# A feed-forward projection in Strassen block products: seven half-width products for eight in 28 of 32 feature tiles

## The chip, the cores and the metric

The kernel runs on one core of one Trainium2 chip. The metric is the device time of one execution in microseconds (us): 1504.65 us before, the median of three runs (1503.68 to 1504.9). Engines are called PE (TensorE matmul), PEld (its weight load), DVE (VectorE), ACT (ScalarE), POOL (GpSimd) and SP (SyncE, which issues the DMAs).

## The reference, cut to what matters

Two layers. Each has adaLN-modulated norms, an input projection, four token mixers and an output projection, and then an MLP with a gated residual. In layer 0 the MLP runs over 512 latent and 256 context tokens, in layer 1 over the 512 latent tokens alone.

```
def channel_mixer(h, w1, w2):          # w1: 1024 x 4096, w2: 4096 x 1024
    return jnp.square(jax.nn.relu(h @ w1)) @ w2

x = x + mod_x[5] * channel_mixer(modulate(rms_norm(x, norm2_g[l]), mod_x[3], mod_x[4]), mlp_w1[l], mlp_w2[l])
if l < DEPTH - 1:
    h_ctx = h_ctx + mod_c[5] * channel_mixer(..., mlp_w1[l], mlp_w2[l])
```

## The kernel before

Activations lie transposed: 128 features on the partitions, the 768 tokens (512 latent, 256 context) as columns. Every product is in fp32 accuracy by three fp32r matmuls (`mm3`, L683): weight high x activation high, weight high x activation low, weight low x activation high. A weight chunk is a 128 x 1024 tile (eight blocks of 128 x 128), loaded as `raw`, cast by ACT to its high part `wh` (L340) and subtracted by DVE to its low part `wl` (L302) in `weight_split` (L656). Three `wh`/`wl` pairs form a ring: the split of a chunk waits until PE has finished with the chunk three before it. Three `raw` tiles exist, two of them for these weights and one for adaLN rows.

`mlp` (L1658) goes over four groups of eight feature tiles of w1. A feature tile is 8 blocks x (512 + 256 columns) x 3 = 48 matmuls into one of two PSUM tiles of the kind `s` (two banks each); in group 0 the first three tiles go third by third (256 tokens each) as the norm delivers them (`together`, L712, names `pair`). `ev_ff` (L1644) takes a tile from PSUM: ReLU and square on ACT (`rl`), the high part `ffh` by a DVE cast (L320) and the low part `ffl` by a DVE subtraction. Then eight output tiles of w2, each over the group's eight `ff` tiles, and `residual` adds each to the stream `x` on DVE, 512 and 256 wide (L307). The last two output tiles of the last group go third by third, so that layer 1's first norm (`norm_third`: `sq`, `st`, `rs`, `rr`, `rb`, then `nu` and `hl` on DVE, `hh` on ACT) starts on third 0 while PE does thirds 1 and 2.

The order of all engines is fixed at build time: `Plan` runs the program's coroutines in a modelled time, and where several want an engine, the lower number in the table `PRIO` goes first. Each engine then executes its list in order. Beside the MLP run the adaLN rows (`ada_row`, `row_work`): a 128 x 1024 row is loaded and reduced on DVE (L594, `dump`) once or twice; those of part 5 of layer 0 (the MLP's gate) wait for the MLP's start (`LATE5 = 1`), the others of layer 1 follow, `ADA_GAP` apart.

Of the kernel before, what the change touches and what calls it, by code (L numbers as in the profile page):

```python
# [238 lines left out]
def hybrid_dit_kernel(  # L239
# [402 lines left out]
    def weight_loader():  # L642
        for i in range(len(order)):
            yield r_raw.get()
            raw = ring.tile([128, D], F32, tag="raw", bufs=N_RAW + N_ARAW, name="raw")
            t = dma(raw, order[i])
            P.spawn(weight_split(i, raw, t))
            while i - state["split"] > 1:
                yield state["split_ev"]
            if i == 1:  # L650
                yield a0_done

# [3 lines left out]
    def weight_split(i, raw, t):  # L656
# [1311 lines left out]
```

## Time and profile before

| | |
|---|---|
| median of three runs | 1504.65 us |
| the profiled execution | 1505.86 us |
| its span, first to last instruction | 1503.5 us (2.4 us lie outside) |
| mean granted TensorE clock | 0.991 |
| PE busy / DVE busy / ACT busy | 1471.1 / 930.6 / 542.2 us |

Busy time is a mean over stages, so it is read by stage: up to 224 us the start and layer 0's projections, to 392 its attention, output projection and first three MLP tiles, to 892 the rest of its MLP, to 924 the turn to layer 1, then the same again. A PE record lasts longer than the distance to the next one, since matmuls overlap; what a matmul costs in a stream is read from starts, or from a long stretch divided by its count. In the same way a DVE record lasts longer than the distance to the next one.

### The profile page before, as it was taken

The page shows a single profiled execution, that of the slowest core. Times are in us where ns is not written, and L with a number is a line of the kernel's source. Part 1 is how long each engine was busy: PE and PEld are TensorE (multiplying, and loading weights), DVE is VectorE, ACT ScalarE, POOL GpSimd, SP SyncE. Part 2 cuts the span into 40 slices and gives each one's busy share as a digit, 9 for nine tenths or more (in the row PEclk, how much of TensorE's full clock was granted, in tenths as well). Part 3 has the DMA queues.
Part 4 walks back from the last instruction along what each step waited for, and adds up shares of the span by engine and source line. Part 5 has one row for each costly group of instructions (what it writes and reads, how often), then busy time and mean ns, then how long its engine had stood idle before and what let it go on. Part 6 is the DMA issues. An engine that isn't in the chain of part 4 may idle for free.

```text
span 1503.5 us, 21831 instructions
## 1 busy us (share of the span) xinstructions
PE 1471.1 (98%) x8692; PEld 1254.8 (83%) x8692; DVE 930.6 (62%) x1631; ACT 542.2 (36%) x941; POOL 78.0 (5%) x94
## 2 busy tenths in 40 slices
PE   8999999999999999999999999999998999999997
PEld 5788887779888888888888899887778888888886
DVE  4899679769755565445443359999767434343343
ACT  4422337655421231132113235327645323132342
POOL 0000002220000000000000000102210000000000
PEclk8999999999999999999999999999999999999999
DMA  9563357211343444444441214545312333333331
GB/s 338 204 236 110 115 173 228 82 30 44 109 130 124 128 125 142 142 152 140 155 140 57 70 43 137 173 144 162 117 57 71 99 98 99 97 92 95 95 98 57
DMA packets 66758, 184.48 MB, mean 123 GB/s; under 512 B 8545, under 2 KB 15457, under 8 KB 66657
## 3 DMA queue, kind: packets, MB, share of 16 engines
q1 hardware_dynamic: 66656, 183.10, 38.0%
q8 instruction: 68, 1.11, 0.3%
q14 instruction: 34, 0.27, 0.1%
HBM read 168.91 MB, written 14.16 MB: 122 GB/s over the span
## 4 chain that ended last, share of the span: by engine, by line
PE 87%; DVE 8%; DMA 2%; issue 1%; SPq 1%; ACT 1%; POOL 0%; DVEq 0%; POOLq 0%; ACTq 0%
PE w L362 65%; PE wo L362 6%; PE pair L362 4%; PE tm L362 3%; PE pv L362 2%; PE tp L1179 2%; DVE wl L302 1%; PE score L362 1%; DMA a<-adaB 1%; DVE ca L307 1%; PE am L437 1%; SPq L368 1%; DVE e L1137 1%; DVE zr L302 1%; DVE x L307 1%
## 5 line engine op out<-in xcount | busy, mean ns | idle before, releaser
L340 ACT CAST wh<-raw 128x1024 fp32r<-128x1024 f32 x184 | 193.2, 1050 | 647.7 <-PE w L362 600.4
L362 PE MATMUL w<-hl,wh 128*128 128x512 f32 (+1 forms) x1072 | 380.1, 355 | 0.5 <-DVE hl L307 0.5
L362 PE MATMUL w<-hh,wh 128*128 128x512 f32 (+1 forms) x1072 | 379.8, 354 | 0.4 <-ACT hh L335 0.4
L362 PE MATMUL w<-hh,wl 128*128 128x512 f32 (+1 forms) x1072 | 378.1, 353 | 0.0
L302 DVE TENSOR_TENSOR wl<-raw,wh 128x1024 fp32r<-128x1024 f32 x184 | 225.0, 1224 | 214.1 <-ACT wh L340 211.1
L362 PE MATMUL w<-ffl,wh 128*128 128x512 f32 (+1 forms) x800 | 277.8, 347 | 0.0
L362 PE MATMUL w<-ffh,wh 128*128 128x512 f32 (+1 forms) x800 | 277.7, 347 | 0.0
L362 PE MATMUL w<-ffh,wl 128*128 128x512 f32 (+1 forms) x800 | 277.6, 347 | 0.0
L362 PEld LDWEIGHTS w<-hh,wh 128*128 128x128 f32 x1072 | 202.8, 189 | 30.5 <-issue 2.1
L362 PEld LDWEIGHTS w<-hl,wh 128*128 128x128 f32 x1072 | 202.8, 189 | 30.0 <-issue 3.0
L362 PEld LDWEIGHTS w<-hh,wl 128*128 128x128 f32 x1072 | 202.6, 189 | 27.2 <-issue 0.2
L307 DVE SCALAR_TENSOR_TENSOR x<-w,md,x 128x512 f32<-128x512 f32 (+1 forms) x100 | 62.1, 642 | 215.6 <-PE w L362 215.5
L362 PEld LDWEIGHTS w<-ffh,wh 128*128 128x128 f32 x800 | 151.5, 189 | 19.1
L362 PEld LDWEIGHTS w<-ffl,wh 128*128 128x128 f32 x800 | 151.5, 189 | 18.9
L362 PEld LDWEIGHTS w<-ffh,wl 128*128 128x128 f32 x800 | 151.4, 189 | 19.0
L594 DVE CUSTOM_DVE_ANT_0 dump<-raw,cbt 128x1024 bf16<-128x1024 f32 x80 | 97.6, 1220 | 19.3 <-DMA raw<-adaT 18.6
L307 DVE SCALAR_TENSOR_TENSOR ca<-gpad,sm,ca 128x783 f32<-128x783 f32 (+1 forms) x120 | 106.8, 890 | 2.3
L345 POOL TENSOR_TENSOR rr<-rs,few 128x2 f32<-128x2 f32 (+1 forms) x30 | 27.3, 911 | 1165.0 <-DVE rs L315 1165.0
L1137 DVE TENSOR_SCALAR_CACHE_REDUCE e<-score 128x768 f32<-128x768 f32 (+1 forms) x80 | 66.1, 846 | 21.5 <-PE score L362 21.2
L335 ACT ACTIVATE e<-e,mx 128x768 f32<-128x768 f32 (+1 forms) x80 | 67.8, 848 | 28.5 <-DVE e L1137 27.4
L362 PE MATMUL wo<-yl,wh 128*128 128x512 f32 (+1 forms) x144 | 53.5, 371 | 2.0 <-DVE yl L302 2.0
L302 DVE TENSOR_TENSOR ffl<-rl,ffh 128x512 fp32r<-128x512 f32 (+2 forms) x73 | 53.7, 742 | 2.1
(165 smaller groups left out, 1892.2 us busy)
## 6 DMA issues: line engine op xcount, KB each, us to landing
raw<-w SPq DMA_DIRECT2D x128, 512.0 KB, 3.6
raw<-adaT SPq DMA_DIRECT2D x56, 512.0 KB, 3.3
raw<-w_in SPq DMA_DIRECT2D x40, 512.0 KB, 4.1
ab<-adaB SPq DMA_DIRECT2D x24, 384.0 KB, 6.4
raw<-wo SPq DMA_DIRECT2D x16, 512.0 KB, 4.0
a<-adaB SPq DMA_DIRECT2D x16, 384.0 KB, 7.2
ks<-qk SPq DMA_DIRECT2D x48, 96.0 KB, 2.2
x<-xT SPq DMA_DIRECT2D x16, 256.0 KB, 5.3
```

The lines of the kernel that those rows point to most:

```text
L302: nc.vector.tensor_tensor(out=out, in0=in0, in1=in1, op=op)
L307: nc.vector.scalar_tensor_tensor(out=out, in0=in0, scalar=s, in1=in1, op0=op0, op1=op1)
L335: nc.scalar.activation(out=out, in_=in_, func=func, scale=scale, **kw)
L340: nc.scalar.copy(out, in_)
L345: nc.gpsimd.tensor_tensor(out=out, in0=in0, in1=in1, op=op)
L362: nc.tensor.matmul(out, lhsT, rhs, start=start, stop=stop)
L368: (eng or nc.sync).dma_start(out=out, in_=in_)
L437: nc.tensor.matmul(pm[32 * j:32 * j + 32, 0:256], sc4[:, j + (0 if first else 4)], raw, start=first, stop=last)
L594: nc.vector.tensor_tensor_reduce(out=dump, in0=raw, in1=cbt[s], op0=ALU.mult, op1=ALU.add, scale=1.0, scalar=0.0, accum_out=md[l][:, s, r: ...
L1137: nc.vector.tensor_scalar(out=e[:, 0:kn], in0=s_[:, k0:k0 + kn], scalar1=-SQ_D, scalar2=None, op0=ALU.mult, op1=ALU.min, accum_out=mx)
L1179: nc.tensor.transpose(tp[:, j * 128:(j + 1) * 128], e[0][:, (k3 + j) * 128:(k3 + j + 1) * 128], id_sb)
```

## The change

In layer 0, 28 of the 32 w1 tiles are taken two at a time. Of a pair, the 8 x 2 weight blocks are cut into four quarters (a11, a12 of one tile, a21, a22 of the other, 4 blocks each), the eight activation tiles and 768 tokens into four quarters of 4 tiles x 384 tokens. Strassen's scheme (in Winograd's form) gives the two feature tiles from seven products of 4 blocks x 384 columns x 3 = 12 matmuls; eight would be needed without sums. In exchange:

- `pair_split`: each pair's weights are four DVE sums of 128 x 512 and seven splits of 128 x 512, made from two raw tiles held at once. Seven halves lie in three and a half ring chunks.
- `sums`: once, during group 0, the activations' four summed quarters per block (`t1`, `t2`, `t3`), with their high and low parts. `t1` replaces the right half of the first four activation tiles after the four plain tiles (`plain_ev`).
- `seven_products`: products 1, 6, 2, 7, 5, 4, 3, each into half a PSUM tile, combined by an ACT copy and seven DVE additions 384 wide (`sum_q` to `sum_c12`); then ReLU, square and the cast to `ffh` on ACT, `ffl` on DVE (`squared`).
- Groups of layer 0 are 4, 6, 6, 6, 6, 4 tiles (`GROUPS`), so its w2 output is added to `x` six times, not four; group 0 is plain. After a group of pairs, the first two output tiles take all but the last two `ff` tiles first.
- Around it: part 5's adaLN rows no longer wait for the MLP (`LATE5 = 0`), `ADA_GAP`, `SLACK`, `CTX_LAG`, `H_KEEP`, the chunk order of both input projections (`W_ORDER`, two rows of number pairs) and nearly all of `PRIO` are different, and a weight's low part is always made on DVE.

```diff
+ADA_GAP = (7000.0, 6000.0, 9000.0, 4500.0, 5500.0)
...
+LATE5 = 0
...
+GROUPS = ((4, 6, 6, 6, 6, 4), (8, 8, 8, 8))
+HALF = NT // 2
...
+    def pair_loader(i, pairs):
...
+            for ap in p:
+                yield r_raw.get()
+                raw = ring.tile([128, D], F32, tag="raw", bufs=N_RAW + N_ARAW, name="raw")
+                two.append((raw, dma(raw, ap)))
+            got.append(two)
...
+            while not got:
+                yield more[0]
+            (r1, t1), (r2, t2) = got.pop(0)
+            a11, a12, a21, a22 = r1[:, 0:512], r1[:, 512:1024], r2[:, 0:512], r2[:, 512:1024]
+            yield t1
+            e11 = yield from half(a11)
+            yield t2
+            yield r_buf.get()
+            s1 = buf([128, 512], name="s1")
+            t = yield from v_tt(s1, a21, a22, ALU.add)
+            yield e11
+            yield from v_tt(a21, a11, a21, ALU.subtract)
+            yield t
+            t = yield from v_tt(a11, s1, a11, ALU.subtract)
+            yield t
+            e6 = yield from half(a11)
+            e12 = yield from half(a12)
+            yield r_buf.get()
+            s4 = buf([128, 512], name="s4")
+            t = yield from v_tt(s4, a12, a11, ALU.subtract)
+            P.spawn(put_after(r_raw, e6, e12, t))
+            yield from half(a21)
+            ev = yield from half(s1)
+            P.spawn(put_after(r_buf, ev))
+            ev = yield from half(a22)
+            P.spawn(put_after(r_raw, ev))
+            yield t
+            ev = yield from half(s4)
+            P.spawn(put_after(r_buf, ev))
...
+    def half_rest(c, o, src, wh, wl, last, ev):
+        t = yield from v_tt(wl, src, bits(wh), ALU.subtract)
+        P.fire(hev[c, o], t)
+        P.fire(ev, t)
...
+    def sums(L):
...
+            yield r_buf.get(2, True)
+            L.t2[k] = [buf([128, NT], F32R, name=nm) for nm in ("t2h", "t2l")]
+            yield r_buf.get(2)
+            u, v = buf([128, NT], name="su"), buf([128, NT], name="sv")
+            t1 = t1s[k // 2][:, (k % 2) * HALF:(k % 2 + 1) * HALF]
+            a, b = L.h2[k], L.h2[k + 4]
+            t = yield from v_tt(u, bits(a.hi), bits(a.lo), ALU.add)
+            tv = yield from v_tt(v, bits(b.hi), bits(b.lo), ALU.add)
+            yield t
+            t = yield from v_tt(t1, u[:, HI], u[:, LO], ALU.subtract)
+            yield max(t, tv)
+            t3 = yield from v_tt(u[:, HI], v[:, HI], u[:, HI], ALU.subtract)
+            t = yield from v_tt(v[:, HI], v[:, HI], t1, ALU.subtract)
+            yield t
+            t = yield from v_tt(v[:, LO], v[:, LO], v[:, HI], ALU.subtract)
+            yield t
+            h, lo = L.t2[k]
+            t = yield from a_copy(h, v)
+            h3, l3 = (x[:, (k % 2) * HALF:(k % 2 + 1) * HALF] for x in L.t3[k // 2])
+            t3 = yield from a_copy(h3, u[:, HI])
+            yield t
+            t = yield from v_tt(lo, v, bits(h), ALU.subtract)
+            for n in (2, 4):
+                P.fire(L.t_ev[k, n], t)
+            yield t3
+            t = yield from v_tt(l3, u[:, HI], bits(h3), ALU.subtract)
+            P.fire(L.t_ev[k, 3], t)
+            r_buf.put(2, t)
+        yield L.plain_ev
+        for k in range(4):
+            t1 = t1s[k // 2][:, (k % 2) * HALF:(k % 2 + 1) * HALF]
+            t = yield from a_copy(L.h2[k].hi[:, HI], t1)
+            yield t
+            t = yield from v_tt(L.h2[k].lo[:, HI], t1, bits(L.h2[k].hi[:, HI]), ALU.subtract)
+            P.fire(L.t_ev[k, 1], t)
+        r_buf.put(2, t)
+
...
+        LO, HI = slice(0, HALF), slice(HALF, NT)
+        h2 = L.h2
+        yield L.sums_ev
+        third = lambda k: slice((k % 2) * HALF, (k % 2 + 1) * HALF)
...
+        def product(p, out):
+            if at["n"] % 2 == 0:
+                at["c"] = chunk()
...
+            yield hev[c, o]
+            wh, wl = wt_[c]
+            for k in range(4):
+                if p in waits:
+                    yield L.t_ev[k, waits[p]]
+                hi, lo = token[p](k)
+                t = yield from mm3(out, wh[:, 4 * o + k], wl[:, 4 * o + k], hi, lo, k == 0, k == 3)
+            if o or at["n"] == 7 * (len(ff) // 2):
+                free_ring(c)
...
+            S.left = {ff[i]: 2, ff[i + 1]: 2}
+            yield r_s.get()
+            p_ = acc_tile("s", "sa")
+            S.a, S.b = p_[:, 0:HALF], p_[:, 512:512 + HALF]
+            yield r_buf.get()
+            S.x = buf([128, NT], name="sx")
+            t = yield from product(1, S.a)
+            P.spawn(sum_p(S), t)
+            t = yield from product(6, S.b)
+            P.spawn(sum_q(S), t)
+            yield r_buf.get(3, True)
+            S.y = buf([128, NT], name="sy")
+            ff[i].make("ff")
+            yield r_acc.get()
+            S.g = acc_tile("acc", "sg")[:, 0:HALF]
+            t = yield from product(2, S.g)
+            P.spawn(sum_c11(S, ff[i]), t)
+            yield r_s.get()
+            p_ = acc_tile("s", "sb")
+            S.c, S.d = p_[:, 0:HALF], p_[:, 512:512 + HALF]
+            t = yield from product(7, S.c)
+            P.spawn(sum_r(S), t)
+            t = yield from product(5, S.d)
+            yield r_buf.get(3, True)
+            S.z = buf([128, NT], name="sz")
+            ff[i + 1].make("ff")
+            P.spawn(sum_c22(S, ff[i + 1]), t)
+            yield r_acc.get()
+            S.e = acc_tile("acc", "sc")[:, 0:HALF]
+            t = yield from product(4, S.e)
+            P.spawn(sum_c21(S, ff[i + 1]), t)
+            yield r_acc.get()
+            S.h = acc_tile("acc", "sh")[:, 0:HALF]
+            t = yield from product(3, S.h)
+            P.spawn(sum_c12(S, ff[i]), t)
+
...
+    def sum_q(S):
+        yield S.ev["p"]
+        t = yield from v_tt(S.x[:, HALF:NT], S.b, S.x[:, 0:HALF], ALU.add)
+        r_s.put(1, t)
...
+    def sum_r(S):
+        yield S.ev["q"]
+        yield S.ev["y"]
+        t = yield from v_tt(S.x[:, 0:HALF], S.c, S.x[:, HALF:NT], ALU.add)
...
+    def sum_c22(S, f):
+        yield S.ev["r"]
+        t = yield from v_tt(S.z[:, HALF:NT], S.d, S.x[:, 0:HALF], ALU.add)
+        P.spawn(rectified(S, S.z, HALF, f), t)
+        t = yield from v_tt(S.x[:, HALF:NT], S.d, S.x[:, HALF:NT], ALU.add)
+        r_s.put(1, t)
+        P.fire(S.ev["u"], t)
...
+    def squared(S, y, o, f):
+        y = y[:, o:o + HALF]
+        t = yield from act(y, y, AF.Square)
+        yield t
+        t = yield from a_copy(f.hi[:, o:o + HALF], y)
+        yield t
+        t = yield from v_tt(f.lo[:, o:o + HALF], y, bits(f.hi[:, o:o + HALF]), ALU.subtract)
+        S.left[f] -= 1
+        if not S.left[f]:
+            r_buf.put(1, t)
+        P.fire(f.ev[0 if o == 0 else 2], t)
+        if not S.left[f]:
+            P.fire(f.ev[1], t)
...
+                cs = [chunk()] if m or not (seven and g) else [chunk(), chunk()]
+                ps = {}
+                cuts = [0, nf] if len(cs) == 1 else [0, nf - 2, nf]
+                for k0, k1 in zip(cuts, cuts[1:]):
+                    for j, c in enumerate(cs):
+                        if c not in ps:
+                            yield wev[c]
```

How this moves instructions, at three places. On PE, at the end of layer 0's group 0, before: the last w1 tile (`w1_4718`) ends and the first w2 output tile begins; the w2 rows run over eight `ff` tiles, of which these are the first three.

```order
L362 MATMUL w1_4718<-hl_4124,wh_4585 128x256
L362 MATMUL w1_4718<-hh_4123,wl_4586 128x256
L362 MATMUL w2_4783<-ffh_4016,wh_4652 128x512
L362 MATMUL w2_4783<-ffl_4017,wh_4652 128x512
L362 MATMUL w2_4783<-ffh_4016,wl_4653 128x512
L362 MATMUL w2_4783<-ffh_4018,wh_4652 128x512
L362 MATMUL w2_4783<-ffl_4019,wh_4652 128x512
L362 MATMUL w2_4783<-ffh_4018,wl_4653 128x512
L362 MATMUL w2_4783<-ffh_4020,wh_4652 128x512
```

The same place on PE now; `w1_4492` is the tile that becomes `ffh_4490` and `ffl_4491`.

```order
L364 MATMUL w1_4492<-hl_4163,wh_4449 128x256
L364 MATMUL w1_4492<-hh_4162,wl_4450 128x256
L364 MATMUL w2_4574<-ffh_4058,wh_4469 128x512
L364 MATMUL w2_4574<-ffl_4059,wh_4469 128x512
L364 MATMUL w2_4574<-ffh_4058,wl_4470 128x512
L364 MATMUL w2_4574<-ffh_4060,wh_4469 128x512
...
L364 MATMUL w2_4574<-ffh_4062,wl_4470 128x512
L364 MATMUL w2_4574<-ffh_4490,wh_4469 128x512
L364 MATMUL w2_4574<-ffl_4491,wh_4469 128x512
```

The tile that has just ended is the eighth of eight before, wanted after 21 matmuls, and the fourth of four now, wanted after 9.

On DVE, at the start of group 1, before: the last output tile of group 0 is added to `x7`, and then come whole weight splits, adaLN rows and a tile's `ffh` and `ffl`.

```order
L307 SCALAR_TENSOR_TENSOR x7_2613<-w2_5222,md0_84,x7_2613 128x512
L307 SCALAR_TENSOR_TENSOR x7_2613<-w2_5222,md0_84,x7_2613 128x256
L302 TENSOR_TENSOR wl_5288<-raw_5181,wh_5287 128x1024
L594 ISA dump_5301,md1_85<-raw_5257,cbt0_80 128x1024
...
L302 TENSOR_TENSOR wl_5352<-raw_5243,wh_5351 128x1024
...
L320 CAST ffh_5284<-rl_5355 128x768
L302 TENSOR_TENSOR ffl_5285<-rl_5355,ffh_5284 128x768
```

The same place on DVE now, from the addition that takes product 2 (`sg`) from PSUM: `raw` and `s` are sums of weight quarters, `hl` from `t1` are the low parts that product 5 reads (one more, `hl_3954`, stands in the row ahead).

```order
L304 TENSOR_TENSOR sy_4941<-sg_4944,sx_4901 128x384
L304 TENSOR_TENSOR s1_4972<-raw_4925 128x512
L304 TENSOR_TENSOR raw_4925<-raw_4893,raw_4925 128x512
L304 TENSOR_TENSOR raw_4893<-s1_4972,raw_4893 128x512
L304 TENSOR_TENSOR hl_3971<-t1_4364,hh_3970 128x384
L304 TENSOR_TENSOR ffl_4943<-sy_4941,ffh_4942 128x384
L304 TENSOR_TENSOR hl_3984<-t1_4654,hh_3983 128x384
L304 TENSOR_TENSOR wl_4992<-raw_4893,wh_4991 128x512 x2
L304 TENSOR_TENSOR s4_4999<-raw_4893 128x512
L304 TENSOR_TENSOR hl_4029<-t1_4654,hh_4028 128x384
```

Three of product 5's four operands now stand behind an addition that waits for product 2, two products ahead of it.

On DVE, at the turn to layer 1, before: from `rs`, which takes the sum of squares of third 0, to the first finished operand `hl` of layer 1.

```order
L315 TENSOR_SCALAR rs_8346<-st_8341 128x2
L307 SCALAR_TENSOR_TENSOR x6_2610<-w2_8321,md0_84,x6_2610 128x256
L302 TENSOR_TENSOR sq_7935<-sq_7935,sq_8365 128x256
L307 SCALAR_TENSOR_TENSOR nu_8377<-x0_2592,gain1_1_87,sq_7933 128x256
L307 SCALAR_TENSOR_TENSOR nu_8387<-x1_2595,gain1_1_87,sq_7933 128x256
L307 SCALAR_TENSOR_TENSOR nu_8397<-x2_2598,gain1_1_87,sq_7933 128x256
L307 SCALAR_TENSOR_TENSOR hl_8376<-nu_8377,md1_85,hh_8375 128x256
```

The same piece of DVE's list now.

```order
L317 TENSOR_SCALAR rs_8997<-st_8990 128x2
L309 SCALAR_TENSOR_TENSOR x7_2661<-w2_8975,md0_84,x7_2661 128x256
L304 TENSOR_TENSOR sq_8730<-sq_8730,sq_9009 128x256
L309 SCALAR_TENSOR_TENSOR nu_9027<-x0_2640,gain1_1_87,sq_8728 128x256
L309 SCALAR_TENSOR_TENSOR x6_2658<-w2_8996,md0_84,x6_2658 128x256
L317 TENSOR_SCALAR rs_9033<-st_9019 128x2
L309 SCALAR_TENSOR_TENSOR nu_9041<-x1_2643,gain1_1_87,sq_8728 128x256
L304 TENSOR_TENSOR wl_9030<-raw_8889,wh_9029 128x1024
L309 SCALAR_TENSOR_TENSOR x7_2661<-w2_9024,md0_84,x7_2661 128x256
L304 TENSOR_TENSOR wl_9064<-raw_8949,wh_9063 128x1024
L309 SCALAR_TENSOR_TENSOR nu_9062<-x2_2646,gain1_1_87,sq_8728 128x256
L309 SCALAR_TENSOR_TENSOR hl_9026<-nu_9027,md1_85,hh_9025 128x256
```

With 4 `ff` tiles in the last group in place of 8, PE's thirds are half as long (24 matmuls, not 48), so the two weight splits and the last residuals now stand ahead of the first `hl`; from the first `nu` to the eighth `hl` of third 0 there are 38 rows: 2 `wl`, 2 `sq` additions, 2 `rs` and 32 of the scalar kind.

## Rows read from the trace of the kernel before

**Rows 1.** The page's first part: each engine's busy time, share of the span and number of instructions.

```profile
PE 1471.1 (98%) x8692; PEld 1254.8 (83%) x8692; DVE 930.6 (62%) x1631; ACT 542.2 (36%) x941; POOL 78.0 (5%) x94
```

**Rows 2.** Busy time by stretch of the span: us from and to, length, then PE, PEld, DVE, ACT and POOL busy us (with counts), granted clock, DMA share, GB/s.

```profile
224.00:392.00 168.00, 164.53 (x1135) 138.72 (x1134) 138.71 (x340) 105.40 (x242) 29.99 (x34) 1.00 0.29 90
392.00:892.00 500.00, 500.00 (x2901) 443.46 (x2900) 249.96 (x369) 115.33 (x140) 0.00 (x0) 1.00 0.39 124
892.00:924.00 32.00, 30.25 (x246) 29.30 (x246) 27.57 (x64) 19.13 (x40) 2.58 (x6) 1.00 0.23 71
924.00:1158.00 234.00, 224.29 (x1357) 186.60 (x1356) 204.10 (x379) 116.59 (x224) 31.92 (x32) 0.98 0.39 122
```

**Rows 3.** The chain that ended last, in order of time (start, us, what): its two longest pieces, the MLPs of layer 0 and layer 1.

```profile
391.91 499.62 PE w L362 x2895
...
1158.40 323.38 PE w L362 x1436
```

**Rows 4.** Instructions by form on PE: the two widths of one of the three w1 matmuls (`w<-hh,wl` and `w<-hl,wh` have the same counts), busy us and mean ns of a record; input projections are counted in.

```profile
L362 PE MATMUL w<-hh,wh 128*128 128x512 f32 x696 | 273.4, 393 | 0.0
L362 PE MATMUL w<-hh,wh 128*128 128x256 f32 x376 | 106.5, 283 | 0.4 <-ACT hh L335 0.4
```

**Rows 5.** Matmuls of 256 columns in order of time (start, us), and from the page's fifth part the weight loads.

```profile
1128.26 0.28 PE L362 MATMUL wo<-ybh,wh 128*128 128x256 f32 x1
1128.38 0.28 PE L362 MATMUL wo<-ybl,wh 128*128 128x256 f32 x1
1128.50 0.28 PE L362 MATMUL wo<-ybh,wl 128*128 128x256 f32 x1
...
L362 PEld LDWEIGHTS w<-hh,wh 128*128 128x128 f32 x1072 | 202.8, 189 | 30.5 <-issue 2.1
```

**Rows 6.** DVE in order of time (start, us, instruction, count, idle time before it and its releaser).

```profile
163.26 1.23 DVE L302 TENSOR_TENSOR wl<-raw,wh 128x1024 fp32r<-128x1024 f32 x1 [0.49 <-ACT wh L340]
164.40 0.69 DVE L307 SCALAR_TENSOR_TENSOR yc<-yth,yc 128x512 f32<-128x512 f32 x1
165.00 0.54 DVE L315 TENSOR_SCALAR yc<-yc,fl 128x512 f32<-128x512 f32 x1
...
172.16 0.41 DVE L302 TENSOR_TENSOR yc<-yc,rb 128x256 f32<-128x256 f32 x1
172.50 0.41 DVE L315 TENSOR_SCALAR yc<-yc,fl 128x256 f32<-128x256 f32 x1
...
419.51 0.56 DVE L320 CAST ffh<-rl 128x768 fp32r<-128x768 f32 x1 [0.36 <-ACT rl L335]
420.11 0.96 DVE L302 TENSOR_TENSOR ffl<-rl,ffh 128x768 fp32r<-128x768 f32 x1
420.99 1.22 DVE L594 CUSTOM_DVE_ANT_0 dump<-raw,cbt 128x1024 bf16<-128x1024 f32 x1
422.13 0.08 DVE L594 DVE_READ_ACCUMULATOR2_ANT md<- 128x1 f32 x1
422.25 1.23 DVE L594 CUSTOM_DVE_ANT_0 dump<-raw,cbt 128x1024 bf16<-128x1024 f32 x1
```

**Rows 7.** PE and ACT around the end of a w1 tile of group 0, in order of time: the next tile's first matmul, and what ACT does.

```profile
416.76 0.40 PE L362 MATMUL w<-hh,wh 128*128 128x512 f32 x1
...
416.84 1.05 ACT L340 CAST wh<-raw 128x1024 fp32r<-128x1024 f32 x1 [5.70 <-PE w L362]
417.80 0.81 ACT L335 ACTIVATE rl<-w 128x768 f32<-128x768 f32 x1
418.63 0.85 ACT L335 ACTIVATE rl<-rl 128x768 f32<-128x768 f32 x1
```

**Rows 8.** The page's sixth part: DMA issues of MLP weights, KB each, median us from issue to landing.

```profile
raw<-w SPq DMA_DIRECT2D x128, 512.0 KB, 3.6
```

**Rows 9.** The turn to layer 1 on DVE, in order of time: the residual of output tile 7, third 0; the first `nu`; and later one `hl` and the next start.

```profile
889.76 0.48 DVE L307 SCALAR_TENSOR_TENSOR x<-w,md,x 128x256 f32<-128x256 f32 x1 [1.49 <-PE w L362]
...
894.39 1.27 DVE L307 SCALAR_TENSOR_TENSOR nu<-x,gain,sq 128x256 f32<-128x256 f32 x3
...
911.76 0.48 DVE L307 SCALAR_TENSOR_TENSOR hl<-nu,md,hh 128x256 fp32r<-128x256 f32 x1
912.15 0.87 DVE L307 SCALAR_TENSOR_TENSOR nu<-x,gain,sq 128x256 f32<-128x256 f32 x2
```

**Rows 10.** The chain that ended last at the end of this turn: the last `pair` piece, and the first piece after it.

```profile
915.72 8.41 PE pair L362 x68
924.13 10.92 PE tm L362 x91
```

**Rows 11.** A wait of PE in layer 1, in order of time (in brackets the idle time), and PE by stretch around it (length, busy, clock, DMA).

```profile
1136.73 0.58 PE L362 MATMUL pair<-hl,wh 128*128 128x256 f32 x1 [3.09 <-DVE hl L307]
1137.11 0.41 PE L362 MATMUL pair<-hh,wl 128*128 128x256 f32 x1
1137.32 0.41 PE L362 MATMUL pair<-hh,wh 128*128 128x256 f32 x1
...
1136.00:1138.00 2.00, 1.27 (x6) 0.55 0.58 123
1138.00:1140.00 2.00, 2.00 (x12) 0.59 0.45 180
```

More of the change, by code (lines that the diff above doesn't have):

```diff
@@ L642, in weight_loader @@
     def weight_loader():
-        for i in range(len(order)):
+        i = 0
+        while i < len(order):
+            if order[i][0] == "pairs":
+                yield from pair_loader(i, order[i][1])
+                i += order[i][2]
+                continue
             yield r_raw.get()
             raw = ring.tile([128, D], F32, tag="raw", bufs=N_RAW + N_ARAW, name="raw")
-            t = dma(raw, order[i])
-            P.spawn(weight_split(i, raw, t))
+            n = 0
+            for ap in order[i]:
+                t = dma(raw[:, n:n + width(ap)], ap)
+                n += width(ap)
+            P.spawn(weight_split(i, raw, t, n))
             while i - state["split"] > 1:
@@ new lines, in pair_split, with half @@
+    def pair_split(i, n, got, more):
+        while state["split"] != i - 1:
+            yield state["split_ev"]
+        at = [0]
+        last = 7 * n
+        def half(src):
+            c, o = i + at[0] // 2, at[0] % 2
+            at[0] += 1
+            if o == 0:
+                yield r_ring.get()
+                wt_[c] = [ring.tile([128, 8, 128], F32R, tag=g, name=g) for g in ("wh", "wl")]
+            wh, wl = (w.rearrange("p k m -> p (k m)")[:, o * 512:o * 512 + 512] for w in wt_[c])
+            t = yield from a_copy(wh, src)
+            ev = Ev()
+            P.spawn(half_rest(c, o, src, wh, wl, at[0] == last, ev), t)
+            return ev
+        for _ in range(n):
+            while not got:
[27 more added lines that the diff above has]
+            P.spawn(put_after(r_buf, ev))
@@ L759, in units_of @@
         wh, wl = wt_[i]
-        return [(wh, wl, j) for j in range(8)]
+        return [(wh, wl, j) for j in range(sum(width(ap) for ap in order[i]) // 128)]
     def acc_tile(kind, name="acc"):
@@ new lines, in add_tile @@
+    def add_tile(L, p_, m, move, fin):
+        new = None
+        if move and 8 - NPAD <= m < 8 - X_PAD:
+            yield r_pad.get()
+            new = pad(f"x{m}")
+        for i, (t0, n) in enumerate(L.segs):
+            lastseg = i == len(L.segs) - 1
+            yield from residual(L, p_, 0, m, t0, n, 5, "s" if lastseg else None, out=new)
+            if new is not None and lastseg:
+                X[m] = new
+                r_buf.put(1, P.clock["dve"])
+                xp["n"] += 1
+            if fin:
+                for q in thirds(t0, n):
+                    P.fire(L.x3[m, q])
@@ L1662, in mlp @@
         full = NL if last else NT
-        for g in range(4):
-            ff = [Act() for _ in range(8)]
+        seven = l == 0
+        for g, nf in enumerate(GROUPS[l]):
+            fin = g == len(GROUPS[l]) - 1
+            ff = [Act() for _ in range(nf)]
             i = 0
-            while i < 8:
+            if seven and g > 0:
+                yield from seven_products(L, ff)
+                i = nf
+            while i < nf:
                 if g == 0 and i == 0:
@@ L1685, in mlp @@
                 i += 1
-            if g == 3:
-                r_buf.put(16, P.clock["pe"])
+            if seven and g == 0:
+                P.fire(L.plain_ev, P.clock["pe"])
+            if fin:
+                r_buf.put(28 if seven else 16, P.clock["pe"])
                 L.x3 = {(m, s): Ev() for m in range(8) for s in range(3)}
```

173 lines of the change are left out of this document (131 added, 42 removed).

## The prediction, made before the changed kernel ran

> **What bounds the kernel now.** I read the shares of the engines first: PE is busy 98% of the span, DVE 62%, ACT 36% [rows 1]. Then the stretches, since the change lies in one stage: from 392 to 892 us, the MLP of layer 0, PE is busy 500.0 of 500 us, DVE 250 and ACT 115 [rows 2]. Then the chain that ended last: in this stretch it is one piece, 499.62 us of PE in 2895 matmuls [rows 3]. So a matmul saved there is time saved, as long as DVE keeps up. DVE is close to its limit only elsewhere: 27.6 of 32 us at the turn to layer 1 and 204 of 234 us after it [rows 2].
>
> **A. The matmuls.** Layer 1's MLP has 512 columns in nearly every matmul: 323.38 / 1436 = 225.2 ns each [rows 3]. Layer 0's has as many of 512 as of 256: 499.62 / 2895 = 172.6 ns on average, so 120.0 for 256 columns, as the starts 0.12 us apart say [rows 3, 5]. (Records last longer, 393 and 283 ns [rows 4], since matmuls overlap; they are no price.) No row has 384 columns. It is bounded by 120.0 and 225.2; two widths lie on a line of 0.41 ns a column and 15 ns a matmul, and I take its middle, 172.6. Removed: 28 tiles x 8 blocks x 3 = 672 matmuls of either width, 672 x 345.2 ns = 232.0 us. Added: 14 pairs x 7 x 12 = 1176, x 172.6 ns = 203.0 us. That is -29.0. In the last group's two output tiles by thirds, 4 `ff` tiles go through 256-wide thirds in place of 8: 48 fewer of 256 and 24 more of 512, -0.3. Together **-29.3 us**, all on the path.
>
> What lies beside it and is costed at nothing: DVE's share of a pair. Its pace is 0.60 us for 512 columns and 0.34 for 256 [rows 6], so 0.47 for 384. Per pair it has 4 sums and 7 low parts of 512 (11 x 0.60) and 7 additions and 4 `ffl` of 384 (11 x 0.47): 11.8 us, in PE time of 84 x 0.1726 = 14.5 us. For two whole tiles it had 2 x (1.14 + 0.60 + 0.88) = 5.2 in 16.6. ACT has 7 casts of 512 and about 13 pieces of 384, at half the 1.05 and 0.83 us of today's [rows 7] some 9.3 us in 14.5. The activation sums, 4 x 5 us of DVE, lie in group 0, where half of DVE's time is free. The two further additions of w2 to `x` (8 tiles each, 0.60 + 0.34) are 15 us, spread over 500. Two raw tiles are now held at once, 512 KB each and 3.6 us from issue to landing [rows 8]; the ring holds four to six half chunks, 8 to 12 us of PE, ahead. POOL gets nothing. If DVE's cover is gone, rival B has the price.
>
> **B. The end of group 0.** It has four tiles. The fourth is wanted by w2 after 9 matmuls of 512 columns, 9 x 0.225 = 2.03 us, where the eighth was wanted after 21, 4.73 us. A tile ends at 416.76 on PE (the next one's first matmul) and its `ffl` at 420.11 + 0.96 = 421.07: 4.3 us, of which ACT takes 1.7 behind a weight cast [rows 6, 7]. Before, 4.73 covered it; now PE waits **+2.3 us** (0 if other work is put in, 4.3 at most).
>
> **C. The first pair.** `t1` is the right half of activations that group 0 still reads, so its low parts are made after it. DVE's list then holds, from the addition that waits for product 2: `sy` 0.47, three sums 1.80, `hl`, `ffl`, `hl` 1.41, two `wl` 1.20, `s4` 0.60, `hl` 0.47, together 5.95 us. Product 5 wants the fourth `hl` 12 x 0.1726 + 9 x 0.1726 = 3.62 us after product 2. So **+2.3 us** (0 to 5). Behind it queue only the rest of this pair; the later ones don't wait.
>
> **D. The turn to layer 1.** PE's work between third 0 and the end of the thirds shrinks by 48 x 0.12 = 5.76 us, which A counts as won; but layer 1 cannot start before DVE is ready. Before: residual of tile 7 at 889.76, first `nu` at 894.39, 4.63 us later; layer 1's first projection, taken by thirds, ends on PE at 924.13, 34.4 us after that residual [rows 9, 10]. Now 38 rows follow the first `nu`: 32 x 0.40 (start to start at 911.76 and 912.15), 2 `wl` at 1.14, 2 `sq` at 0.34 and 2 `rs` at 0.07, 15.9 us. Then PE has 9 matmuls of the last block and 72 of the second third, 81 x 0.12 = 9.7 us. That is 4.63 + 15.9 + 9.7 = 30.3, so 4.1 us are won and not 5.76: **+1.7 us** (0 to 5.8).
>
> **E. The clock.** After a wait of 3.09 us in layer 1 the granted clock is 0.55 and 0.59, the lower level, and matmuls of 256 columns start 0.21 us apart instead of 0.12 [rows 5, 11]; some 13 such, 13 x 0.09 = 1.2 us. B or C may do the same once: **+1.2 us** (0 to 2.4).
>
> **F. What moves around it.** Part 5's adaLN rows, 16 reductions of 1.26 us [rows 6], go from the MLP into the attention stage: 20.2 us of DVE where 168 - 138.7 = 29.3 are idle [rows 2]. PE idles 3.5 us there and 9.7 from 924 to 1158 [rows 2], and the order of both stages is new, by changed priorities. Such an order can win a part of these 13 us, or make DVE late. No row prices it; between -5 and +5 I take **+1.0 us**.
>
> **Sum.** -29.3 + 2.3 + 2.3 + 1.7 + 1.2 + 1.0 = -20.8. The profiled execution took 1505.86 (span 1503.5 and 2.4 outside), so 1485.1; it is 1.2 above the median of the runs, so **1484 us**, with ends of 1480 and 1491 by the bounds of B to F, which will not all fall on one side.
>
> **Rivals.** *No losses*: the turns are covered, and the new order wins back what B to E cost. 1504.65 - 29.3 = 1475. For it: PE waits hardly at all before, with just such turns. Against: B's and C's lists are in the order as it stands.
>
> *DVE falls behind within the pairs.* 11.8 of 14.5 us is 81%; DVE also has reductions (1.26 us) between, and its list is in order, so an addition that waits for a product holds all behind it. By the records' lengths (0.69 for 512, 0.55 for 384) a pair with one reduction is 11 x 0.69 + 11 x 0.55 + 1.27 = 14.9 us, over 14.5. That is 0.4 us over with one reduction and 1.7 with two; at 0.8 us in each of 14 pairs it adds 11 us: 1495. For it: from 924 to 1158 DVE is at 87%, and PE idles 4% there. Against: starts are 0.60 apart for 512, so the records overlap.
>
> *The weight load sets the pace.* A load is busy 189 ns [rows 5]. If no matmul could go faster than its load, 1176 x 0.189 = 222 us would be needed, A would be -10, and with the same losses the time 1503, no change. Against: matmuls of 256 columns, each with a load of its own, start 120 ns apart [rows 5]. The Trainium skill, TensorE: Matmul & The Clock Gate, section Back-to-back issue gap, says that load and matmul set the spacing together, some 81 ns at 128 columns and 131 at 512. As an estimate from that page, A would be 672 x 229 - 1176 x 114 = 20 us, not 29; the trace disagrees, with 225 ns at 512 columns.
>
> *Slower: DVE's list waits at each addition.* It must wait for the product's end, and each such wait may cost the handover that a row shows, 0.49 us [rows 6]. Then a pair costs 11.8 + 1.26 + 7 x 0.49 = 16.5 us; it decides from 14.5 + (29.3 - 8.5) / 14 = 16.0, where a pair has lost what A wins less B to F. 14 x 0.5 over that is +7: 1512 us. Against: PE is ahead of DVE in most of the seven products, so the product is often there before DVE comes to it.
>
> That the change does not do what it says is excluded: the order has 1176 matmuls of 384 columns in layer 0.
>
> **Chances.** The forecast 0.55, no losses 0.17, DVE behind within the pairs 0.20, weight load 0.03, slower 0.05. About 2 in 10 may lie outside the range, so it runs from 1474 (no losses) to 1496 (most of DVE behind). 0.2%, 3 us, is about what a measurement of this kernel can tell from no change. Faster by more: 0.55 + 0.17 + 0.20 = 0.92; the same, 0.03; slower, 0.05.
>
> **What would show it.** In the chain, the MLP's PE piece should hold matmuls of 384 columns about 173 ns apart; 189 or more speaks for the weight load. PE should wait once for `ffl` at the end of group 0, once for `hl` in the first pair and once for layer 1's first `hl`, 2 to 3 us each; waits for `ffh`, `wl` or the additions' PSUM tiles in every pair speak for DVE falling behind, as does DVE busy over 95% there. The granted clock should be lower just behind such waits and nowhere else. The attention stage should keep its 168 us within 5; a stage after 924 that is some 10 us longer or shorter would make F the largest error. The forecast is wrong if PE waits in most of the 14 pairs, or if the three turns cost nothing.

## The result, and where the time went

The changed kernel takes 1520.55 us (median of 4 runs, 1520.03 to 1521.43) where the kernel before takes 1504.16: ratio 1.0111, 95% interval 1.0093 to 1.0128. It is 16 us slower. The forecast was 1484 us and faster. A few us between two runs are read beside their clocks, for executions of one kernel differ by that much: `e1_places`, below, took 1495.65 us at a mean granted clock of 0.992 and 1501.36 at 0.986.

The page's first part of the changed kernel, beside [rows 1]: PE has 15.5 us less to do, as forecast in kind, in a span that is 15.0 us longer.

```profile
PE 1455.6 (96%) x8500; PEld 1253.4 (83%) x8500; DVE 1067.1 (70%) x1939; ACT 621.2 (41%) x1165; POOL 84.5 (6%) x94
```

Its chain that ended last, beside [rows 3, 10] (start, us, what): the first w1 tile after the thirds, the end of the turn to layer 1 and the first piece behind it, layer 1's MLP.

```profile
394.71 6.95 PE w L364 x37
...
924.56 8.66 PE pair L364 x70
933.22 10.92 PE w L364 x48
...
1173.65 323.38 PE w L364 x1436
```

These marks cut each run into stages. "Start" is the first whole-tile w1 matmul of layer 0, "MLP and turn" goes from there to the first piece behind the turn, "between" from there to the 323.38 us of layer 1's MLP, which is the same in every run. The stages are those of each run's profiled execution, the medians are over all its executions.

| run | median us | start | MLP and turn | between |
|---|---|---|---|---|
| before | 1504.16 | 391.74 | 532.39 | 234.27 |
| changed | 1520.55 | 394.55 | 538.67 | 240.43 |
| e1_places | 1496.76 | 393.61 | 519.73 | 235.68 |
| e2_first | 1507.56 | 392.95 | 526.63 | 239.20 |
| e3_oldtab | 1560.03 | 392.38 | 582.86 | 240.87 |
| e4_newtab | 1507.31 | 394.05 | 532.54 | 234.43 |
| e5_late | 1490.13 | 394.92 | 512.69 | 234.61 |
| e6_turns | 1507.53 | 393.76 | 530.55 | 237.33 |
| e7_groups | 1498.46 | 394.93 | 519.53 | 238.35 |
| e8_stages | 1512.51 | 402.80 | 520.67 | 241.11 |
| e9_save | 1486.20 | 393.26 | 512.59 | 233.27 |
| e10_save_only | 1512.48 | 395.85 | 538.57 | 232.60 |
| e11_move1 | 1491.38 | 394.93 | 514.31 | 233.79 |
| e12_groups | 1481.38 | 395.48 | 508.51 | 230.41 |

So the change loses 2.8 us before the MLP, 6.3 in the MLP and its turn, where the prediction's terms A to E promised -21.8, and 6.2 between the MLPs. Most of the error is in the MLP. There, the chain through one ordinary pair of the changed kernel reads:

```profile
572.26 2.44 PE sa L364 x14
574.71 0.02 issue
574.73 0.49 ACT sx L342
575.22 0.04 issue
575.26 2.01 PE sa L364 x10
577.27 2.08 PE sg L364 x12
579.35 2.45 PE sb L364 x14
581.79 0.02 issue
581.82 0.57 DVE sx L304
582.38 0.04 issue
582.43 2.01 PE sb L364 x10
584.43 2.08 PE sc L364 x12
586.51 2.08 PE sh L364 x12
```

Three products run undisturbed at 2.08 us, 173 ns a matmul. But `sa` and `sb`, which hold two products each, break after 14 of 24 matmuls: 12 of the first product, two of the second, then PE stands until ACT or DVE has read the first product out. (In some pairs the break comes a few matmuls later.) The same place in order of time (PE and ACT; in brackets the idle time and its releaser), where product 6 begins at 574.18:

```profile
574.01 0.33 PE L364 MATMUL sa<-hh,wl 128*128 128x384 f32 x1
574.18 0.33 PE L364 MATMUL sa<-t2h,wh 128*128 128x384 f32 x1
574.35 0.34 PE L364 MATMUL sa<-t2l,wh 128*128 128x384 f32 x1
574.73 0.48 ACT L342 COPY sx<-sa 128x384 f32<-128x384 f32 x1 [0.64 <-PE sa L364]
...
575.26 0.45 PE L364 MATMUL sa<-t2h,wl 128*128 128x384 f32 x1 [0.57 <-ACT sx L342]
575.54 0.34 PE L364 MATMUL sa<-t2h,wh 128*128 128x384 f32 x1
```

ACT starts only when the second matmul of product 6 has ended, though it needs only product 1; and the third matmul starts only when ACT has ended, though it reads nothing of ACT's. Both waits are the program's own: in the trace the second matmul of product 6 raises the semaphore that ACT's copy waits for, and the third matmul waits for the one that the copy raises. From 574.35 to 575.54 two matmuls take 1.19 us, not 0.35: 0.84 us lost. At product 5 it is 0.92 (581.44 to 582.71). What PE waited for in all from 390 to 935 us (total, times, longest):

```profile
PE sa L364 <- ACT sx L342: 8.0, 14, 0.6
PE sb L364 <- DVE sx L304: 7.8, 12, 0.7
PE pair L364 <- DVE hl L309: 2.9, 3, 2.1
PE w L364 <- DVE x L309: 2.3, 2, 1.2
PE sb L364 <- DVE hl L304: 2.0, 2, 1.5
PE w L364 <- DVE ffh L322: 0.9, 1, 0.9
PE w L364 <- DVE ffl L304: 0.5, 1, 0.5
```

26 such waits, the first two rows (the expectations below count 28), 14 x 0.84 + 12 x 0.92 = 22.8 us.

### The profile page after: what moved, and what is told of

It is laid out like the page before. It is cut to its first block, busy times and chain, and to the rows that moved or that the text cites. A ratio compares the mean times of both kernels' runs of the same rounds, so it can differ in the third digit from the quotient of the medians.

```text
span 1518.5 us, 22138 instructions
## 1 busy us (share of the span) xinstructions
PE 1455.6 (96%) x8500; PEld 1253.4 (83%) x8500; DVE 1067.1 (70%) x1939; ACT 621.2 (41%) x1165; POOL 84.5 (6%) x94
## 4 chain that ended last, share of the span: by engine, by line
PE 67%; DVE 11%; ACT 1%; issue 1%; DMA 1%; POOL 1%; DVEq 0%; POOLq 0%; ACTq 0%
PE w L364 40%; PE wo L364 6%; PE sa L364 4%; PE pair L364 4%; PE sb L364 3%; DVE wl L304 2%; PE sc L364 2%; PE sh L364 2%; DVE ca L309 2%; PE sg L364 2%; PE pv L364 1%; PE score L364 1%; PE tp L1282 1%; DVE x L309 1%; DVE nu L309 1%
## 5 line engine op out<-in xcount | busy, mean ns | idle before, releaser
L342 ACT CAST wh<-raw 128x1024 fp32r<-128x1024 f32 (+2 forms) x242 | 208.8, 869 | 495.3 <-PE w L364 403.0
L304 DVE TENSOR_TENSOR wl<-raw,wh 128x1024 fp32r<-128x1024 f32 (+2 forms) x242 | 240.6, 1001 | 128.6 <-ACT wh L342 125.1
L364 PE MATMUL w<-hh,wh 128*128 128x512 f32 (+1 forms) x624 | 230.4, 369 | 0.7 <-ACT yu L342 0.7
L364 PE MATMUL w<-hl,wh 128*128 128x512 f32 (+1 forms) x624 | 229.6, 368 | 0.3 <-DVE hl L309 0.3
L364 PE MATMUL w<-hh,wl 128*128 128x512 f32 (+1 forms) x624 | 229.3, 367 | 0.0
L309 DVE SCALAR_TENSOR_TENSOR x<-w,md,x 128x512 f32<-128x512 f32 (+1 forms) x132 | 83.6, 635 | 182.2 <-PE w L364 181.7
L364 PEld LDWEIGHTS w<-hh,wl 128*128 128x128 f32 x624 | 118.3, 190 | 21.6 <-issue 3.3
L364 PEld LDWEIGHTS w<-hh,wh 128*128 128x128 f32 x624 | 118.2, 190 | 21.1 <-issue 2.1
L364 PEld LDWEIGHTS w<-hl,wh 128*128 128x128 f32 x624 | 118.3, 190 | 20.0 <-issue 1.6
L364 PE MATMUL wo<-yh,wh 128*128 128x512 f32 (+1 forms) x144 | 53.6, 372 | 1.4 <-ACT zr L342 1.4
```

The source lines that it names most:

```text
L304: nc.vector.tensor_tensor(out=out, in0=in0, in1=in1, op=op)
L309: nc.vector.scalar_tensor_tensor(out=out, in0=in0, scalar=s, in1=in1, op0=op0, op1=op1)
L342: nc.scalar.copy(out, in_)
L364: nc.tensor.matmul(out, lhsT, rhs, start=start, stop=stop)
```

## The theories

The letters here are those of the theories; the prediction's A to F are called its terms.

**A.** The two halves of an `s` tile are kept apart by program waits: a read of one half waits for the matmuls into the other half that were issued ahead of it, and matmuls behind it wait for the read. The planner issues the copy of product 1 some 0.2 us after that product's end in its model, that is behind two matmuls of product 6. **B.** DVE and ACT are late in the pairs, wherever the products lie. **C, F.** The new tables cost time around the MLP (C in e3 and e4, F in e8). **D**, in e5: two products in one tile cost time by themselves, whenever they are read. (G is below; the "Theory D" of e12 is term D.)

A sign of A stood in the trace of before, in the w1 tiles that go third by third in one `s` tile (PE and ACT in order of time, at the ends of the first and of the second third):

```profile
372.33 0.38 ACT L335 ACTIVATE rl<-pair 128x256 f32<-128x256 f32 x1 [0.66 <-PE pair L362]
372.76 0.38 PE L362 MATMUL pair<-hh,wl 128*128 128x256 f32 x1 [0.53 <-ACT rl L335]
```

```profile
382.45 0.38 ACT L335 ACTIVATE rl<-pair 128x256 f32<-128x256 f32 x1 [1.19 <-PE pair L362]
382.88 0.38 PE L362 MATMUL pair<-hh,wl 128*128 128x256 f32 x1 [0.47 <-ACT rl L335]
```

After two matmuls of the next third PE stood 0.53 and 0.47 us for ACT's read of the last one. The `s` tile has 1024 columns in two banks, so the first step, from columns 0 to 255 to 256 to 511, stays in one bank; the second, to 512 to 767, goes to the other bank, as the two products do, and it is the closer sign. Such waits came four times, 2.1 us in all, off any list of the costliest groups.

## Experiments on the pairs

**e1_places** and **e2_first**: the places of products 6 and 2 are exchanged, and (e1 alone) those of 5 and 4 in the same way.

```diff
-            S.a, S.b = p_[:, 0:HALF], p_[:, 512:512 + HALF]
+            S.a, S.g = p_[:, 0:HALF], p_[:, 512:512 + HALF]
...
+            yield r_acc.get()
+            S.b = acc_tile("acc", "sg")[:, 0:HALF]
             t = yield from product(6, S.b)
...
-            yield r_acc.get()
-            S.g = acc_tile("acc", "sg")[:, 0:HALF]
             t = yield from product(2, S.g)
```

> The changed kernel with two PSUM places exchanged, nothing else: product 6 goes to the single-bank tile that product 2 had and product 2 to the second half of product 1's tile; product 5 and product 4 likewise. Theory A (a reader of one half of a PSUM tile makes the matmuls into the other half wait): the 28 waits of PE for sx disappear, 14 x (0.85 + 0.93) = 24.9 us, so about 1495.6 us, and a pair takes 14.5 to 14.8 us in place of 16.3. Rival B (DVE and ACT are late within the pairs, wherever the products lie): the waits come back on other matmuls of the pair, 1512 to 1521 us.

> Only the first of the two exchanges (products 6 and 2). Theory A: the waits for ACT's sx go, those for DVE's sx stay: 14 x 0.85 = 11.9 us, about 1508.6 us. Rival B: within 3 us of the changed kernel, 1518 to 1521.

e1: 1496.76 us (ratio 0.9955, 0.9942 to 0.9968). e2: 1507.56 (1.0021, 1.0011 to 1.0032). In e2's trace the 14 waits for ACT's `sx` are gone and the 12 for DVE's are there, 7.8 us as before; in e1's both are gone, with 2.9 us of new waits for `sx` in four places. Stage MLP and turn: -12.0 us in e2, -18.9 in e1, and the times are close to A's 1508.6 and 1495.6. B falls: the same additions on the same engines cost far less from other places.

**e5_late**: places as in the changed kernel; only the moment at which the reader is issued moves.

```diff
             t = yield from product(1, S.a)
-            P.spawn(sum_p(S), t)
             t = yield from product(6, S.b)
+            P.spawn(sum_p(S), t)
...
             t = yield from product(7, S.c)
-            P.spawn(sum_r(S), t)
             t = yield from product(5, S.d)
+            P.spawn(sum_r(S), t)
```

> The changed kernel with its PSUM places as they are, but the copy sx of product 1 is issued only after product 6, and the addition sx of product 7 only after product 5. Theory A (the wait comes from the reader being issued while the other half of its tile is still being written): the 28 waits go although the places are shared, 1495 to 1499 us, since the additions come 2 us later. Rival D (two products in one tile cost time by themselves, whenever they are read): 1512 us or more.

1490.13 us (0.9902, 0.9880 to 0.9925), better than expected: besides the 26 waits, both waits for `hl` in the first pair and one of the two of 1.16 us for `x` are gone. Its chain through a pair is PE alone, 14.56 us (549.91 to 564.47), and in that stretch (length; PE, PEld, DVE, ACT, POOL busy; clock, DMA) DVE's records fill 13.9 of it:

```profile
549.91 4.16 PE sa L364 x24
554.07 2.08 PE sg L364 x12
556.15 4.16 PE sb L364 x24
560.31 2.08 PE sc L364 x12
562.39 2.08 PE sh L364 x12
```

```profile
549.91:564.47 14.56, 14.56 (x85) 14.56 (x85) 13.91 (x26) 9.02 (x19) 0.00 (x0) 1.00 0.24 78
```

A is shown from both sides: another tile, or another moment, and the wait is gone; the additions come 2 us later and nobody minds. D falls: the two products still share a tile. The prediction's two rivals in which DVE sets the pace are out: DVE keeps up, if narrowly. The Trainium skill, PSUM — Partial Sum Buffer, section Terms, says that a bank is 2 KiB a partition and that two engines in one bank (and one quadrant of its partitions) at once are an error. 2 KiB are 512 fp32, so by this rule columns 0 and 512 of a tile lie in two banks and need no such wait. No run here reads one half while the other is written, so whether the chip would bear it stays open: the wait alone was not taken away.

## Experiments around the pairs

**e3_oldtab, e4_newtab, e8_stages**: the tables of before on the changed kernel, those of the change on the kernel before, and e1 with the old tables of the stages outside the MLP alone (LATE5 = 0 kept).

```diff
-LATE5 = 0
+LATE5 = 1
...
-CTX_LAG = 3
+CTX_LAG = 2
```

> The changed kernel with the tables of before: PRIO for all names that both have, W_ORDER, ADA_GAP, SLACK, CTX_LAG, H_KEEP and LATE5 = 1. Rival C (the re-ordered stages around the MLP cost about 9 us: 2.8 before the MLP and 6.2 between MLP and MLP): about 1511.5 us, with the 28 waits still there. Theory A alone (the tables are worth nothing): 1520.

> The kernel before with the tables of the change and the old MLP, without block products. Rival C: about 9 us slower than before, 1513 us. Theory A alone: 1504 us, the tables cost nothing.

> e1_places with the tables of before for the stages outside the MLP alone: W_ORDER, SLACK, CTX_LAG, H_KEEP and the priorities of projections, attention and norms; LATE5 = 0, ADA_GAP and the priorities of weights, adaLN rows, ff and residual stay as the change has them. Theory F (the new tables cost 1.9 us before the MLP and 1.4 us between the MLPs of e1_places): 1493.5 us. Rival (the tables fit the new MLP, and the old ones don't): 1497 or more.

e3: 1560.03 us (1.0375, 1.0360 to 1.0391), far off both expectations. One wait of PE is the reason:

```profile
452.65 0.79 PE L364 MATMUL w<-ffh,wh 128*128 128x512 f32 x1 [39.75 <-DVE x L309]
```

A group of four reaches its first addition to `x` a group of eight's half earlier, and that addition needs the gate, part 5's adaLN rows; with LATE5 = 1 they are only then being loaded (DVE waits 12.2 us in five places for them, 395 to 460 us). So LATE5 = 0 belongs to the smaller first group, and e3's total says nothing of the other tables; but its stage between the MLPs is 240.87 us with the old tables too. e4: 1507.31 (1.0022, 1.0011 to 1.0032), 3 us and not 9: start +2.3, between +0.2. e8: 1512.51 (1.0046, 1.0031 to 1.0062), 16 us over e1, of it 9.2 before the MLP, so its rival held. The tables are no loss of 9 us; with the rows moved to the attention stage they are what keeps it short, at about 2.3 us. The 6.2 us between the MLPs have another cause.

**e6_turns**: e1 with terms B and C attacked. **e7_groups**: e1 with a last group of six.

```diff
-                cs = [chunk()] if m or not (seven and g) else [chunk(), chunk()]
+                cs = [chunk()] if m or not seven else [chunk(), chunk()]
...
-'sums': 28
+'sums': 3
```

```diff
-GROUPS = ((4, 6, 6, 6, 6, 4), (8, 8, 8, 8))
+GROUPS = ((4, 4, 6, 6, 6, 6), (8, 8, 8, 8))
```

> e1_places with two turns covered: at the end of group 0 the first two output tiles take the first two ff tiles first (the fourth is wanted some 4.8 us after its end, not 2.0), and the priority number of sums goes from 28 to 3, so the low parts hl of t1 come ahead of the next pair's weight sums. Theory (terms B and C as the trace of e1_places has them: 0.94 + 0.49 and the spacing behind them, 1.85; 0.82 + 0.31 + 1.66 = 2.8): 4.6 us less than e1_places, about 1492. Rival (DVE is the bound there, the wait moves to the next thing that it is late with): 1495 to 1498.

> e1_places with the groups (4, 4, 6, 6, 6, 6): the last group has six ff tiles, so PE's thirds are 36 matmuls and not 24. Theory (term D: at the turn DVE's list is late because PE's thirds are short): the wait of 2.35 us for the first hl and the low clock behind it shrink, 1494 to 1495.5 us. Rival (the turn is set by DVE's list, whatever PE does): 1496.8.

e6: 1507.53 us (1.0010, 0.9999 to 1.0021), 11 us over e1. The waits for `hl` in the first pair went, and larger ones came in group 0, one of 2.47 us for ACT's `rl` (408.30) and this one:

```profile
421.56 0.79 PE L364 MATMUL w<-ffh,wh 128*128 128x512 f32 x1 [3.72 <-DVE x L309]
```

The wait moved, as the rival says, and cost some 10 us more than its 1495 to 1498. In the changed kernel's group 0 (402 to 438 us) DVE is already busy 34.9 of 36 us, the prediction's "half of DVE's time is free" was wrong, and what is pulled forward there delays `ff` and `x`. e7: 1498.46 (0.9944, 0.9924 to 0.9964), no gain over e1 in the median. In the profiled execution (1499.44 us) the wait for the first `hl` at the turn went, but the granted clock fell to 0.50 from 451.37 to 461.61 us, at the first pair's waits; MLP and turn is 0.2 us shorter, between 2.7 longer. Two of its five executions, with mean clocks of 0.992 and 0.991, took 1494.86 and 1494.04 us, as the theory expects, so e7 does not decide.

**e9_save, e10_save_only, e11_move1**: theory G. In group 0, `add_tile` moves `x3` and `x4` into two of the five `pad` buffers, where `x5` to `x7` lie anyway (`if move and 8 - NPAD <= m < 8 - X_PAD`). At the turn layer 1's convolution needs `pad` buffers for `gpad` and `ca`, and gets them when `x` has been saved. POOL in the changed kernel:

```profile
940.71 0.11 POOL L1054 MEMSET gpad<- 128x15 f32 x1 [23.89 <-DMA xsave<-x]
...
942.96 0.11 POOL L1054 MEMSET gpad<- 128x15 f32 x1 [2.05 <-DMA xsave<-x]
```

In the trace of before the two memsets stand at 907.6 and 938.5, the first 16.5 us ahead of the turn's end; now it is 7.5 us behind it. So in the first 30 us behind the turn DVE is busy 19.6 us (columns as above; 29.1 before), and the convolution ends in front of the attention, where PE waits for the softmax's `e`:

```profile
933.22:963.22 30.00, 29.32 (x138) 24.25 (x137) 19.56 (x28) 11.02 (x17) 2.05 (x7) 1.00 0.55 184
```

```profile
1024.29 1.01 PE L364 MATMUL score<-ks,qs 96*128 96x512 f32 x2 [4.79 <-DVE e L1240]
```

e9 and e10 change the order of the saves, on e5 and on the changed kernel; e11, on e5, moves one tile of `x`.

```diff
-        for k in range(8):
+        for k in (5, 6, 7, 3, 4, 0, 1, 2):
             t = dma(xsave[:, k], X[k][:, 0:NL])
```

```diff
-        if move and 8 - NPAD <= m < 8 - X_PAD:
+        if move and 8 - NPAD < m < 8 - X_PAD:
```

> e5_late with one more edit: at the turn to layer 1 the tiles of x are saved to memory in the order 5, 6, 7, 3, 4, 0, 1, 2 in place of 0 to 7. Theory G (five tiles of x sit in the five pad buffers now, three before, so gpad waits for the sixth save, and the convolution starts late and ends in front of the attention): gpad's memset comes some 10 us earlier, DVE fills the first 30 us after the turn (20.0 us busy in e5_late), the wait of 5.0 us for e goes, 1484 to 1487 us. Rival (DVE has time enough for the convolution later; the wait has another cause): 1490 us.

> The changed kernel with this edit alone (the order of the saves), the 28 waits kept. Theory G: the time from the turn to the second MLP was 6.2 us longer than before; 4 to 6 us of it go, 1514 to 1517 us. Rival: 1520 us.

> e5_late with one tile of x moved to a pad buffer in group 0 in place of two (x4 alone), the saves in the old order. Theory G: one pad buffer is free for the first gpad at the turn, 1485 to 1488 us. Rival (the buffer that x3 now keeps is missing in the pairs, and they wait): over 1491 us.

e10: 1512.48 us (1.0047, 1.0032 to 1.0062), 8 us less than the changed kernel for this edit alone, all of it between the MLPs (240.43 to 232.60) and more than the 4 to 6 expected; the wait for `e` is 1.80 us there. e9: 1486.20 (0.9871, 0.9856 to 0.9886), as expected; its first memset comes at 899.59, and DVE is busy 26.1 of the first 30 us behind the turn. But on e5 the stage is only 1.3 us shorter (234.61 to 233.27), though e5 had the same wait for `e`, 5.0 us. What sets e5 apart is the granted clock. The stage between the MLPs (columns as above) in the changed kernel, before, in e10 and in e5:

```profile
933.22:1173.65 240.43, 226.03 (x1358) 189.99 (x1357) 203.87 (x380) 117.24 (x226) 31.78 (x35) 0.96 0.38 123
924.13:1158.40 234.27, 224.56 (x1358) 186.87 (x1357) 204.37 (x379) 116.83 (x224) 31.92 (x32) 0.98 0.39 122
934.42:1167.02 232.60, 222.16 (x1357) 187.04 (x1357) 202.09 (x380) 116.79 (x226) 33.55 (x32) 0.99 0.39 127
907.61:1142.22 234.61, 220.95 (x1357) 186.36 (x1357) 202.88 (x380) 117.26 (x226) 33.60 (x35) 0.99 0.38 124
```

PE idles 14.4 us in the changed kernel, 9.7 before, 10.4 in e10 and 13.7 in e5. So e5 idles nearly as long as the changed kernel, but PE is busy 5.1 us less with the same matmuls. In the changed kernel the clock is 0.50, the lower of its two levels, three times for 6.8 us: at the wait for `e` (1023.84 to 1030.66), behind one of 2.38 us for `yl` (1071.62 to 1078.45) and around two of 1.78 and 1.47 us (1150.13 to 1156.96). In e5 this happens once, at the wait for `e`, in e10 once, before twice for 10.2 us in all. So e10 shows that the order of the saves can take the changed kernel's 6.2 us away, and e5, with the saves in the old order, that the late convolution alone does not cost them: the longer waits and the lower clock behind them do it together. Why the second and third of these stretches are not in e5 is not settled.

e11: 1491.38 (0.9906, 0.9890 to 0.9923), no gain, against the theory's expectation; the rival's time came, but not by its waits in the pairs: one free buffer holds the first `gpad`, memset at 891.4, but the first `ca` is still at 923.5 (923.3 in e5), for the second `gpad` waits for a save until 919.30; the convolution needs two buffers.

**e12_groups**: e9 with e7's groups.

> e9_save with the groups (4, 4, 6, 6, 6, 6). In e7_groups the wait for the first hl at the turn went, but the run was no faster than e1_places. Theory D: without the other waits the turn's 2.1 us and the low clock behind it are won now, 1483.5 to 1485. Rival (as in e7_groups, the time is given back behind the turn, where DVE has the convolution): 1486 or more.

1481.38 us (0.9855, 0.9837 to 0.9873), the fastest, and 2 us under its expectation: 22.1 us under the kernel before in its job, e9 18.8 in its own; their intervals overlap, so the step from e9 is not settled. MLP and turn is 4.1 us shorter, and the granted clock stays at 1.00 at the turn.

## Why the prediction was wrong

**Term A held.** 1176 matmuls of 384 columns at 173 ns (2.08 / 12) against 172.6 forecast, and a pair is 14.56 us of PE when nothing stops it, against 14.5.

**Terms B to E were of the right size.** B: 0.94 + 0.49 us of waiting, some 2.0 with the wider spacing behind it, forecast 2.3. C: 0.52 + 1.48 of waiting, some 2.9 in the same way, forecast 2.3. D and E: from the first `nu` to the end of the turn 25.6 us were forecast (15.9 + 9.7), and it is 933.22 - 906.59 = 26.6, 29.7 before [rows 9, 10], with the lower clock in it. DVE's first `nu`, PE's wait, and the stretch around it (columns as above):

```profile
906.59 0.49 DVE L309 SCALAR_TENSOR_TENSOR nu<-x,gain,sq 128x256 f32<-128x256 f32 x1 [0.64 <-ACT sq L342]
```

```profile
911.44 0.58 PE L364 MATMUL pair<-hl,wh 128*128 128x256 f32 x1 [2.07 <-DVE hl L309]
```

```profile
910.00:912.00 2.00, 0.56 (x2) 0.56 (x3) 2.00 (x5) 0.82 (x3) 0.00 (x0) 0.80 0.75 147
912.00:914.00 2.00, 2.00 (x12) 2.00 (x11) 2.00 (x7) 0.91 (x2) 0.00 (x0) 0.50 1.04 416
```

Without its 22.8 us the changed kernel would win 16.5 us in MLP and turn (22.8 - 6.3); A to E said 21.8. Two waits of 1.16 us for DVE's `x` are a part of the rest and were not forecast. e5 wins 19.7 us there, since C's waits and one of these are gone too.

**The step that failed** is the one after term A, "What lies beside it and is costed at nothing: DVE's share of a pair". The additions' time was counted and rightly found to be hidden; that a read from PSUM can stop the matmuls beside it was not asked. Two products lie in one tile, the diff says so (`S.a, S.b = p_[:, 0:HALF], p_[:, 512:512 + HALF]`), and each read of a first half cost 0.84 or 0.92 us, 22.8 in all. The semaphores say it too: two matmuls into product 6 there is a wait on ACT, at a matmul whose operands come from elsewhere.

**Term F was mis-sized**, +1.0 against 2.8 before the MLP and 6.2 between the MLPs. The first is mostly the tables with the moved rows (2.3 in e4). The second is not the tables (0.2) but comes with the two tiles of `x` in `pad` buffers, a part of the diff that the prediction did not price: a new wait of POOL for a DMA, off every engine that was looked at, then PE's wait for `e`, and 20.5 us at the lower clock where the kernel before has 10.2; term E allowed one such drop, behind B or C.

The rival that came nearest in time, 1512 by a handover of 0.49 us at each addition, had the wrong engine: not DVE waited at seven additions, but PE at one copy by ACT and at one of DVE's additions. The forecast's own sum is near what the scheme gives without the two new waits: e9 takes 1486.2 us, with 1484 forecast. That is in part luck: C's waits are gone there, and the stage between the MLPs is 1.0 us shorter than before, while F's +1.0 stood for a loss.

## What to carry to other kernels

When a step puts two results into one PSUM tile, ask when the first is read: if while the second is being written, price one read plus its handover for PE, or read it after both, or place the two that are adjacent in time in different tiles. When buffers change hands (here two tiles of `x` in another pool), follow who next takes one of that pool, however far down the program. And look for the signature of a new wait in the old trace by form, not by total: one row of 0.47 us told it.

## What was not expected of the hardware

The 26 short waits of 0.57 to 0.65 us did not lower the granted clock: it is 1.00 in the pairs, and also around term C's waits of 0.52 and 1.48 us (448 to 454 us). But the length of the last wait does not decide alone: e1 and e7 have the same waits for `hl` there, 0.65 and 1.49 us, and the clock stayed at 1.00 in e1 (451 to 461 us) and was 0.50 in e7. Behind the turn's 2.07 us it went to 0.50, and in e6 it is 0.89 on average over group 0 (402 to 449 us), which has the waits of 2.47 and 3.72 us. The first two matmuls behind a short wait also start further apart, 0.28 us in place of 0.17.
